# Output transposes of a hybrid attention and delta-rule block: on VectorE, between stores and 128-byte loads, instead of on TensorE

## The chip, the core and the metric

The kernel runs on one core of one Trainium2 chip. A core has five engines that run at the same time, each through its own list of instructions: TensorE (PE, matmuls), VectorE (DVE), ScalarE (ACT), GpSimd (POOL) and SyncE (SP, which issues the DMAs here). They hand work to each other through semaphores, and 16 DMA engines move data between HBM and the on-chip memory (SBUF: 128 partitions; matmuls write to PSUM). The metric is the device time of one execution in microseconds (us); of several runs the median is given.

## The reference

One block of a model: T = 1024 tokens of width D = 1024, all in float32. The normalized input is projected to the inputs of 8 heads of stick-breaking attention (64 wide) and of 4 heads of a gated delta rule (128 wide). Each head's output is normalized, multiplied by a gain and by a gate, and all go through one output projection, to which the input is added. A last norm ends it.

```python
h = rmsnorm(x, norm1_w[layer])
proj = jnp.einsum('btd,de->bte', h, w_in[layer])
sb_q, sb_k, sb_v, sb_z, g_q, g_k, g_v, g_z, g_b, g_a = jnp.split(proj, split_idx, axis=-1)
o_sb = stick_breaking_attention(...)
o_sb = rmsnorm(o_sb.transpose(0, 2, 1, 3), sb_norm_w[layer]).reshape(b, t_len, SB_WIDTH)
o_sb = o_sb * jax.nn.silu(sb_z)
...
o_gdn = gated_delta_chunked(gq, gk, gv, decay, beta)
o_gdn = rmsnorm(o_gdn.transpose(0, 2, 1, 3), gdn_norm_w[layer]).reshape(b, t_len, GDN_WIDTH)
o_gdn = o_gdn * jax.nn.silu(g_z)
mixed = jnp.concatenate([o_sb, o_gdn], axis=-1)
x = x + jnp.einsum('bte,ed->btd', mixed, w_out[layer])
...
return rmsnorm(x, final_norm_w)
```

## The kernel before, in words

**Matmuls.** A float32 product is made of three matmuls of the faster type `fp32r`: each operand is split in a high and a low half, and high x high, low x high and high x low are summed in PSUM (`mm3`). ACT makes a high half by copying to fp32r, DVE or POOL the low half by subtracting. A matmul of 128 x 512 results is the unit of nearly all work.

**Stages.** (1) The projections run through 24 groups of columns in the order of `ORDER`; they are the fill work of the whole span up to the last 60 us. (2) The delta rule (`gdn_*`): 4 heads, 8 chunks of 128 tokens; a unit is a head and half of its chunks (g = 0 or 1). `gdn_chain` walks the chunks of a unit one after the other, since each needs the state that the chunk before it left. Its output for a chunk is copied out of PSUM by ACT (`goe`) and stored to the DRAM array `og_s`; the factor of its norm is kept in `rsg`. (3) Attention (`window`): a head's queries in 4 windows w of 256. At a window's end the output lies in PSUM transposed (the head's 64 columns along the partitions, in two partial sums one above the other): ACT and DVE bring both halves together in `o2`, two transposes on PE turn it (`otf`), DVE's `tensor_reduce` adds the two partial sums (`oe`), and one DMA stores it to `o_s` in runs of 256 bytes. (4) The output projection runs over 8 blocks b of 128 tokens, first the delta rule's half (`products_delta`, blocks d0 to d7), then attention's (`products_attention`, a0 to a7): per block 2 halves of 512 columns x 4 rows of weights (k = 0 to 3) x 3 matmuls, so 24.

**A block's input.** `enter_delta` loads a block from `og_s` and its gate from `gate_s` into a place of `kq`, and scales each head by `rsg` on DVE (4 instructions). `enter_attention` loads from `o_s`, and norms with a square (ACT), a reduce (DVE), a power (POOL) and a product (DVE, by `rsb`). `prepare` and `split` then turn the block with 4 transposes on PE (`mwf`), multiply by the gate on DVE (`mf`), and make the halves `mh` (ACT) and `ml` (POOL). The product is added to the residual rows `xr` on DVE.

**The last weights.** `out_rows` loads the raw weight rows (`wor`) for both halves of the projection into the places sg1 and sg2 that attention's windows have left; `weight` makes `woh` (ACT) and `wol` (DVE) of them. The four rows of attention's half are made by `out_weights_attention` while the projection is under way.

**What sets the order.** The kernel is written as streams (Python generators with a priority, lines 1613 to 1619). At build time `interleave` runs them against a cost model of the engines (`Model`); at each point the ready stream with the lowest number emits its next piece. The order in which an engine begins its work in this model is then fixed by dependencies (line 1621), so PE, DVE, ACT, POOL and the DMA queue of SP all run through a list that the build has set. `flags` name events of the plan (`d3`: the add of the delta rule's block 3 was emitted; `e73`: the store of head 7's window 3). `Fixed` holds places in SBUF that several tensors use one after the other: sg0 to sg3, `o2`, and four of 4096 bytes per partition, `kq`. Every engine instruction goes through one helper, so the profile has them all at L359, and names tell them apart.

## Time and profile before

| | |
|---|---|
| runs of the kernel before | 640.44, 641.15, 641.22 us; median 641.15 |
| the profiled execution | 641.73 us, of it the span 639.8 us |
| instructions in the span | 11363 |
| DMA over the span | 116.01 MB, mean 181 GB/s |
| packets under 512 bytes | 53952 of 127162 |
| clock granted to PE | 9 of 9 tenths in 39 slices of 40, 8 in the last |

The span is what the profiler saw between the first and the last instruction; the execution's own time is 1.93 us longer. The rows that the prediction shows come from five views: the busy times and the chain that ended last (on the page), the waits of an engine (who waited for whom: total, times, longest), groups of like instructions (busy us, mean ns of one, then idle time before them and what ended it), the timeline (start, duration, instruction) and windows (busy time of each engine in a stretch, then the clock granted to PE, the DMA share and GB/s). DMA rows tell packets, MB and the share of the time of 16 engines; an issue row tells the count, the KB of one and the us from issue to landing.

### The profile page before, as it was taken

What the parts mean: (1) busy time and instruction counts of PE and PEld (TensorE: products, weight loads), DVE (VectorE), ACT (ScalarE), POOL (GpSimd) and SP (SyncE); (2) the same over time, 40 slices, a digit from 0 to 9 for tenths busy, and PEclk for the clock granted to TensorE, in tenths of its full rate; (3) what the DMA queues carried; (4) which work ended last, traced back from release to release, by engine and by line L of the source; (5) the groups of instructions that cost most, each with busy time, mean ns of one, the idle gap of its engine ahead of it and who ended that gap; (6) DMA issues with size and microseconds to landing.
All of it is one profiled execution on the core that took longest, in us unless ns stands there. A gap on an engine that the chain in (4) does not pass through costs nothing.

```text
span 639.8 us, 11363 instructions
## 1 busy us (share of the span) xinstructions
PE 630.5 (99%) x3768; PEld 536.1 (84%) x3768; DVE 443.1 (69%) x818; ACT 394.3 (62%) x945; POOL 340.3 (53%) x429
## 2 busy tenths in 40 slices
PE   8999999999999999999999999999999999999995
PEld 7889988998888888878888878888888888888885
DVE  4369973322797877886787868577878877567854
ACT  5755567724786776766687674575678753222553
POOL 0124047828694596865497763777353532246432
PEclk9999999999999999999999999999999999999998
DMA  8967338866456437787449674434253289833132
GB/s 296 352 204 288 121 133 255 284 214 211 137 151 232 121 91 221 172 222 240 123 115 256 177 226 125 139 113 167 77 161 98 81 288 358 309 99 98 67 131 100
DMA packets 127162, 116.01 MB, mean 181 GB/s; under 512 B 53952, under 2 KB 93056, under 8 KB 127104
## 3 DMA queue, kind: packets, MB, share of 16 engines
q1 hardware_dynamic: 126816, 115.09, 57.0%
q8 instruction: 30, 0.49, 0.3%
q14 instruction: 28, 0.23, 0.1%
q10 hardware_dynamic: 288, 0.20, 0.1%
HBM read 78.12 MB, written 37.13 MB: 180 GB/s over the span
## 4 chain that ended last, share of the span: by engine, by line
PE 90%; DVE 3%; ACT 3%; POOL 1%; DMA 1%; issue 1%; POOLq 0%; DVEq 0%; ACTq 0%; SPq 0%
PE pp L359 54%; PE pz L359 25%; PE po L359 7%; PE pc L359 3%; DMA cb<-cum_s 1%; DVE cc L359 1%; DVE pp L359 1%; ACT pre L359 1%; DMA n<-n 1%; ACT pz L359 0%; POOL ac L359 0%; DVE ahl L359 0%; POOL dt L359 0%; DVE ac L359 0%; ACT sgf L359 0%
## 5 line engine op out<-in xcount | busy, mean ns | idle before, releaser
L359 PE MATMUL pp<-xh,weh 128*128 128x512 f32 x360 | 145.8, 405 | 0.0
L359 PE MATMUL pp<-xh,wel 128*128 128x512 f32 x360 | 141.2, 392 | 0.0
L359 PE MATMUL pp<-xl,weh 128*128 128x512 f32 x360 | 140.6, 391 | 0.0
L359 POOL TENSOR_TENSOR sgf<-sgf,cc 128x128 f32<-128x128 f32 (+3 forms) x64 | 77.2, 1211 | 60.1 <-DVE cc L359 57.4
L359 POOL TENSOR_TENSOR wel<-wer,weh 128x512 fp32r<-128x512 f32 x48 | 63.3, 1321 | 47.8 <-ACT weh L359 47.6
L359 PEld LDWEIGHTS pp<-xh,wel 128*128 128x128 f32 x360 | 67.6, 188 | 15.2
L359 PEld LDWEIGHTS pp<-xh,weh 128*128 128x128 f32 x360 | 67.6, 188 | 12.1
L359 PEld LDWEIGHTS pp<-xl,weh 128*128 128x128 f32 x360 | 67.8, 188 | 11.8
L359 DVE TENSOR_TENSOR_SCAN cc<-pz,step 128x384 f32<-128x384 f32 (+2 forms) x64 | 53.5, 847 | 14.6 <-ACT pz L359 10.6
L359 ACT ACTIVATE sgf<-pz,rs 128x384 f32<-128x384 f32 (+3 forms) x96 | 53.6, 591 | 2.8 <-PE pz L359 2.5
L359 DVE TENSOR_TENSOR ahl<-pz,ahl 128x512 fp32r<-128x512 f32 (+1 forms) x80 | 49.6, 630 | 3.9 <-ACT ahl L359 3.3
L359 ACT ACTIVATE pz<-pz,ns 128x384 f32<-128x384 f32 (+3 forms) x96 | 52.1, 571 | 0.0
L359 ACT ACTIVATE ahl<-pz 128x512 fp32r<-128x512 f32 (+1 forms) x80 | 43.0, 557 | 12.1 <-PE pz L359 11.6
L359 PE MATMUL po<-ahl,v2a 128*128 128x512 f32 (+1 forms) x160 | 49.2, 402 | 0.0
L359 POOL TENSOR_TENSOR ml<-mf,mh 128x512 fp32r<-128x512 f32 x16 | 21.8, 1360 | 48.0 <-ACT mh L359 48.0
L359 POOL TENSOR_TENSOR ac<-ac,pre 128x512 f32<-128x512 f32 x24 | 30.9, 1289 | 27.3 <-ACT pre L359 24.2
L359 DVE SCALAR_TENSOR_TENSOR pp<-pre,conv,pp 128x512 f32<-128x512 f32 x42 | 31.5, 749 | 18.0 <-ACT pp L359 17.7
L359 DVE TENSOR_TENSOR_SCAN cc<-pz,cc,step 128x512 f32<-128x512 f32 (+1 forms) x32 | 38.8, 1212 | 5.4 <-ACT pz L359 4.2
L359 PE MATMUL pp<-wo,mh 128*128 128x512 f32 x128 | 40.7, 399 | 0.0
L359 PE MATMUL pz<-kh,q 128*128 128x384 f32 (+3 forms) x96 | 36.0, 382 | 0.1
L359 PEld LDWEIGHTS pz<-step,stf 128*128 128x128 f32 x288 | 30.8, 141 | 5.5 <-DVE cc L359 0.6
L359 ACT ACTIVATE weh<-wer 128x512 fp32r<-128x512 f32 x48 | 30.4, 636 | 5.8 <-PE pp L359 2.6
(302 smaller groups left out, 1571.2 us busy)
## 6 DMA issues: line engine op xcount, KB each, us to landing
wer<-wE SPq DMA_DIRECT2D x48, 256.0 KB, 3.3
xr<-x SPq DMA_DIRECT2D x16, 512.0 KB, 6.5
g_s<-ac SPq DMA_DIRECT2D x20, 256.0 KB, 2.2
v_s<-v2e SPq DMA_DIRECT2D x16, 256.0 KB, 3.0
kqf<-g_s SPq DMA_DIRECT2D x16, 256.0 KB, 3.6
v2a<-v_s SPq DMA_DIRECT2D x8, 512.0 KB, 4.2
q<-qk_s SPq DMA_DIRECT2D x8, 512.0 KB, 5.7
kh<-qk_s SPq DMA_DIRECT2D x8, 512.0 KB, 4.3
```

Source lines behind the costliest of these rows:

```text
L359: ins = f(*args, **kw).ins
```

## The change

- **Window's end.** The two PE transposes and the reduce go. DVE turns `o2` in 32 x 32 blocks (one instruction, 128 x 256), and four stores of 32 partitions each put the blocks in their transposed places in `o_s`, in runs of 128 bytes. Both partial sums are stored, side by side; `o_s` is twice as large.
- **`out_norm`, new.** Two streams share the 8 blocks. A block (512 KB) is loaded once all windows of the last head are stored, into the place of sg3, which is cut in two; DVE adds the partial sums, ACT squares, DVE reduces, POOL takes the power, DVE multiplies and turns in 32 x 32 blocks, and a store in runs of 256 bytes puts it to `on_s`.
- **`enter_attention`.** Four loads in runs of 128 bytes from `on_s` bring a block in transposed form; the norm is done already.
- **Delta rule.** `gdn_chain` copies its output into the unit's own place in `kq`; at the unit's end DVE scales all four chunks (one instruction) and turns them into the place of `kn`, and four stores in runs of 128 bytes write `og_s` in transposed form. `enter_delta` loads it as it is, without scaling; its first four blocks may come when the chain of unit 6 (units are 0 to 7) is done (flag c6), the others after the last chain (g).
- **`split`.** No transposes; the gate is multiplied in place, and `mh` and `ml` go to a place of `ak` (four of them; three buffers before).
- **Places.** `kn` and `at` share a place of the new fixed set `ak`, 4 x 4096 bytes.
- **Rules of the streams.** A raw row of attention's weights is loaded only after flags d1 to d4; the residual rows wait for d0 on (from the fourth block); the sigmoid and the product of `g_evac` get another priority, and so do `enter_x` and `out_norm`.

```diff
@@ window
-            op = pz()
-            ot = fx.words(o2, "ot")
-            for i in range(2):
-                TE.transpose(op[:, i * P:(i + 1) * P].bitcast(F32R), ot[:, i * P:(i + 1) * P], idr)
-            oe = at_.tile([P, 2, SBD], F32, tag="oe", bufs=2, name="oe")
-            V.tensor_reduce(oe, op[:, 0:256].rearrange("p (i u d) -> p i d u", i=2, u=2), AX.X, ALU.add)
-            flags[f"e{h}{w}"] = S.dma_start(o_s[2 * w:2 * w + 2, :, h * SBD:(h + 1) * SBD].rearrange("b t d -> t b d"), oe)
+            oe = at_.tile([P, 256], F32, tag="oe", bufs=2, name="oe")
+            V.transpose(oe, o2)
+            rows_o = o_s[256 * w:256 * w + 256, h].rearrange("(b r) d -> r b d", r=32)
+            flags[f"e{h}{w}"] = [S.dma_start(rows_o[:, :, 32 * a:32 * a + 32], oe[32 * a:32 * a + 32].rearrange("r (b c) -> r b c", c=32)) for a in range(4)]
...
+        def out_norm(n):
+            yield lambda: f"e{SBH - 1}3" in flags and fx.room("sg3")
...
+                both = fx.tile([P, SBH, 2, SBD], F32, "both", "sg3")
+                ck.hold(both)
+                yield S.dma_start(both.rearrange("p h u d -> p (h u d)"), o_s[b * P:(b + 1) * P].rearrange("t h d -> t (h d)"))
+                o, spare = both[:, :, 0, :], both[:, :, 1, :]
+                V.tensor_tensor(o, o, spare, ALU.add)
+                A.activation(spare, o, AF.Square)
...
+                V.tensor_tensor(o, o, ss.unsqueeze(2).to_broadcast([P, SBH, SBD]), ALU.mult)
+                V.transpose(spare, o)
+                ck.free(both)
+                flags[f"o{b}"] = S.dma_start(on_s[b].rearrange("p (n d) -> p n d", d=SBD), spare)
@@ gdn_chain
-                    oe = gd.tile([P, P], F32, tag="goe", bufs=2, name="goe")
-                    A.activation(oe, ob, AF.Copy)
-                    S.dma_start(og_s[c, :, h, :], oe)
+                    A.activation(og[:, j, :], ob, AF.Copy)
...
-            st["done"] = rsqrt(rsg[:, h, 4 * g:4 * g + 4], sso, 4)
+            st["done"] = rsqrt(rsg, sso, 4)
+            V.tensor_tensor(og, og, rsg.unsqueeze(2).to_broadcast([P, 4, P]), ALU.mult)
+            V.transpose(ogt, og)
+            for a in range(4):
+                ks = slice(32 * a, 32 * a + 32)
+                S.dma_start(og_s[4 * g:4 * g + 4, :, h, ks].rearrange("c (b r) t -> r (c b) t", r=32), ogt[ks].rearrange("r c (b t) -> r (c b) t", t=32))
+            ck.free(kq, kn, nkv)
@@ out_rows
-                    yield lambda: fx.room(f"sg{1 + n % 2}")
+                    yield lambda: fx.room(f"sg{1 + n % 2}") and (n < 4 or f"d{n - 3}" in flags)
@@ split
-            tp = pz()
-            mw = fx.words(mg, "mw")
-            yield from turned(tp, [mw[:, 0, j * P:(j + 1) * P] for j in range(4)])
-            fv = pools[0].tile([P, 512], F32, tag="mf", name="mf")
-            V.tensor_tensor(fv, tp, gt.rearrange("p k t -> p (k t)"), ALU.mult)
+            fv = mg[:, 0, :]
+            V.tensor_tensor(fv, fv, gt.rearrange("p k t -> p (k t)"), ALU.mult)
+            mm = fx.tile([P, 2, 4, P], F32R, "mm", "ak")
@@ enter_delta
-            yield lambda: "pool0" in flags and "z7" in flags
+            yield lambda: "z7" in flags
...
-                yield lambda: fx.room("kq")
+                yield lambda: ("c6" if b < 4 else "g") in flags and fx.room("kq")
...
-                for g in range(GH):
-                    gs = slice(g * P, (g + 1) * P)
-                    r = V.tensor_scalar(mx[:, gs], mx[:, gs], rsg[:, g, b:b + 1], None, ALU.mult)
@@ enter_attention
-                S.dma_start(mx, o_s[b])
...
+                for j in range(4):
+                    r.append(S.dma_start(mx[32 * j:32 * j + 32].rearrange("p (k a c) -> p k a c", k=4, a=4), heads[j]))
```

How the built order moves, at three places. VectorE, at the split of the last weight rows (`wol3`), before: `pp_7016` and `pp_7030` are the two halves of delta block 3, `pp_7082` is the first half of block 4.

```order
L359 SCALAR_TENSOR_TENSOR wol2_7000<-worf169_6896,mixw_67,woh2_6999 128x1024
L359 TENSOR_TENSOR xr_6859<-pp_7016,xr_6859 128x512
L359 TENSOR_TENSOR xr_6859<-pp_7030,xr_6859 128x512
L359 TENSOR_TENSOR mf_7076<-pz_7070,mgf167_6821 128x512
L359 SCALAR_TENSOR_TENSOR wol3_7041<-worf173_6994,mixw_67,woh3_7040 128x1024
L359 TENSOR_TENSOR xr_6861<-pp_7082,xr_6861 128x512
```

The same place of the change: `pp_7102` is the second half of the last delta block, d7, and `pp_7116` the first half of a0, the first block that uses `wol3`; `mgf169` and `mgf171` are inputs of attention's blocks, `bothf170` is a block of `out_norm`.

```order
L363 TENSOR_TENSOR xr_6991<-pp_7102,xr_6991 128x512
L363 TENSOR_TENSOR mgf169_6979<-mgf169_6979 128x512
L363 TENSOR_TENSOR mgf171_7000<-mgf171_7000 128x512
L363 TENSOR_TENSOR bothf170_6985<-bothf170_6985 128x8x64
L363 TENSOR_REDUCE oss_7136<-bothf170_6985 128x8
L363 TENSOR_SCALAR oss_7136<-oss_7136 128x8
L363 SCALAR_TENSOR_TENSOR wol3_7150<-worf172_7027,mixw_67,woh3_7149 128x1024
L363 TENSOR_TENSOR bothf170_6985<-bothf170_6985,oss_7136 128x8x64
L363 STREAM_TRANSPOSE bothf170_6985<-bothf170_6985 128x8x64
L363 TENSOR_TENSOR xr_6700<-pp_7116,xr_6700 128x512
```

`wol3` has moved from between blocks 3 and 4 of the delta half to behind its last add, and the first steps of a block of `out_norm` stand ahead of it. On ScalarE `woh3` stands right behind the square of the same `bothf170`.

SyncE's DMA queue, up to the load of the last weight rows (`worf173`), before: `mgf` with `og_s` and `gate_s` are a delta block's input, `fnw` is the final gain.

```order
L359 DMA xr_6867<-x 128x1024
L359 DMA gate_s_91<-zt_6852 128x512
L359 DMA worf169_6896<-wo 128x1024
L359 DMA mgf171_6924<-og_s_95 128x512
L359 DMA mgf171_6924<-gate_s_91 128x4x128
L359 DMA fnw_6964<-fnw 128x1024
L359 DMA worf173_6994<-wo 128x1024
```

And of the change, where the last weight rows are `worf172`:

```order
L363 DMA bothf166_6950<-o_s_94 128x1024
L363 DMA mgf167_6955<-gate_s_91 128x4x128
L363 DMA mgf167_6955<-on_s_95 32x16x32 x4
L363 DMA mgf169_6979<-gate_s_91 128x4x128
L363 DMA mgf169_6979<-on_s_95 32x16x32
L363 DMA xr_6991<-x 128x1024
L363 DMA mgf169_6979<-on_s_95 32x16x32 x3
L363 DMA mgf171_7000<-gate_s_91 128x4x128
L363 DMA mgf171_7000<-on_s_95 32x16x32 x4
L363 DMA bothf170_6985<-o_s_94 128x1024
L363 DMA worf172_7027<-wo 128x1024
```

The last weight rows now stand behind the residual rows of block 7 (`xr_6991`), inputs of attention's first blocks and two loads of `out_norm`.

TensorE, near the end of the delta rule, before: a window's end, between matmuls of the delta rule (`vr`, `pc`) and of attention's values (`po`).

```order
L359 MATMUL pz_6424<-state_6248,kqf89_4636 128x128
L359 MATMUL pz_6424<-vr_6315,at_4748 128x128
L359 MATMUL pz_6431<-step_65,otf145_6432 128x128 x2
L359 MATMUL po_6438<-ahl_6295,v2a_6326 128x512 x2
L359 MATMUL po_6438<-ahl_6403,v2a_6326 128x512
```

A like place of the change, where the last part of a window (`ahl` with `v2a`) is followed by a projection.

```order
L363 MATMUL pz_6455<-state_6374,kqf82_4270 128x128
L363 MATMUL pz_6455<-vr_6413,akf83_4273 128x128
L363 MATMUL pc_6469<-state_6436,kqf96_4732 128x128
L363 MATMUL po_6368<-ahl_6425,v2a_6113 128x512
L363 MATMUL po_6368<-ahl_6425,v2a_6113 128x2x128
L363 MATMUL pp_6484<-xh_112,weh_6327 128x512
```

The transposes with `otf`, as those with `mwf`, are gone from the list. Behind the delta rule's last matmul 27 projection matmuls stand before the first of the output projection; before there were 90.

79 lines of the change are left out of this document (43 added, 36 removed).

## The prediction

> **What bounds the kernel now.** First the page's busy times and the chain that ended last, then the waits of TensorE (PE).
>
> ```profile
> PE 630.5 (99%) x3768; PEld 536.1 (84%) x3768; DVE 443.1 (69%) x818; ACT 394.3 (62%) x945; POOL 340.3 (53%) x429
> PE 90%; DVE 3%; ACT 3%; POOL 1%; DMA 1%; issue 1%; POOLq 0%; DVEq 0%; ACTq 0%; SPq 0%
> PE po L359 <- DVE step L359: 1.7, 1, 1.7
> PE pp L359 <- DVE v2e L359: 0.4, 1, 0.4
> 616.38 16.81 PE pp L359 x84
> ```
>
> PE is busy for 630.5 of 639.8 us. Of the 9.3 us it is not, 1.7 lie at the start, and 6.6 at the end: the last row of PE in the chain of waits runs from 616.38 to 633.2, and the span ends at 639.8. The second largest wait is 0.4. So the kernel is as long as PE's list of instructions plus a fixed head and tail: a matmul that goes is worth its time on PE in full, work added to another engine is worth nothing until PE waits for it, and each wait that appears counts in full. The profiled execution took 641.73 us, 1.93 more than its span and 0.58 more than the median; I sum against 641.73 and take off the 0.58 at the end.
>
> **What the change removes from PE.** The durations of pipelined matmuls overlap, so I count from start to start.
>
> ```profile
> 507.68 0.37 PE L359 MATMUL pz<-step,otf 128*128 128x128 f32 x2
> 507.89 0.46 PE L359 MATMUL pp<-xh,weh 128*128 128x512 f32 x1
> 508.18 0.39 PE L359 MATMUL pp<-xl,weh 128*128 128x512 f32 x1
> 508.41 0.39 PE L359 MATMUL pp<-xh,wel 128*128 128x512 f32 x1
> ...
> 586.70 0.46 PE L359 MATMUL pz<-step,mwf 128*128 128x128 f32 x4
> 587.00 0.46 PE L359 MATMUL pp<-woh,mh 128*128 128x512 f32 x1
> 587.30 0.39 PE L359 MATMUL pp<-wol,mh 128*128 128x512 f32 x1
> ...
> 521.05 0.29 PE L359 MATMUL pz<-step,otf 128*128 128x128 f32 x2
> 521.17 0.50 PE L359 MATMUL pz<-step,mwf 128*128 128x128 f32 x4
> L359 PE MATMUL pz<-step,otf 128*128 128x128 f32 x64 | 11.4, 260 | 0.0
> L359 PE MATMUL pz<-step,mwf 128*128 128x128 f32 x64 | 7.4, 238 | 0.0
> ```
>
> A pair of attention's transposes (otf) takes 0.21 (507.68 to 507.89), and the matmul behind it 0.29 (to 508.18) where its neighbour takes 0.23 (508.18 to 508.41): 0.27 a pair, and the 64 of the group are 32 pairs, 8.6. Four transposes of a block's input (mwf) take 0.30, and the matmul behind them 0.30 instead of 0.23: 0.37, 16 times, 5.9. Together 14.5. Where the two kinds stand side by side, as at 521.05, the late start of a next matmul is counted twice; I take off 0.5: **−14.0**. The busy times of the groups (11.4 + 7.4 = 18.8) overlap with their neighbours and would be too much.
>
> **What it adds elsewhere.** VectorE (DVE):
>
> ```profile
> L359 DVE STREAM_TRANSPOSE wc<-xc 128x256 f32<-128x256 f32 x4 | 1.7, 428 | 0.0
> L359 DVE STREAM_TRANSPOSE pre<-ac 128x512 f32<-128x512 f32 x12 | 8.5, 707 | 5.4 <-POOL ac L359 5.4
> L359 DVE TENSOR_REDUCE oe<-pz 128x128 f32<-128x256 f32 x32 | 13.3, 416 | 2.6 <-PE pz L359 2.5
> L359 DVE TENSOR_SCALAR mgf<-mgf,rsg 128x128 f32<-128x128 f32 x32 | 8.0, 312 | 0.0
> L359 DVE TENSOR_TENSOR mgf<-mgf,rsb 128x512 f32<-128x512 f32 x8 | 7.7, 961 | 7.3 <-POOL rsb L359 7.3
> L359 DVE TENSOR_TENSOR xr<-pp,xr 128x512 f32<-128x512 f32 x31 | 21.3, 686 | 14.6 <-PE pp L359 14.3
> ```
>
> The window's transpose of 256 elements (0.43) takes the place of the reduce (0.42). New are 16 transposes of 512 elements (0.71), 8 adds of the two partial sums and 8 scalings of the delta rule's output (0.69 to 0.96 each); the 32 scalings by rsg (8.0) go. That is 11.4 + 11 to 15 − 8.0, some 15 to 20 us on an engine that is idle for 200, spread over the span beside PE: I cost it at nothing there. ScalarE and GpSimd (POOL) keep their counts. The sync engine (SP) issues some 136 more DMAs (128 stores of a window instead of 32, 32 loads of attention's output instead of 8, and a load and a store of the sums for each block); during attention nothing on PE waits for them soon, since the sums are first read in the last 60 us. If that cover is gone, what it costs is a wait of PE at the output projection, which I now work out.
>
> **What becomes late.** In the changed order only 27 projection matmuls stand between the delta rule's last matmul and the output projection, where 90 stood before; 63 x 0.23 = 14.5 us of cover are gone while the list of transfers is longer.
>
> ```profile
> 520.00:560.00 40.00, 40.00 (x191) 32.78 (x190) 26.17 (x54) 13.87 (x19) 10.82 (x8) 1.00 0.94 335
> 560.00:600.00 40.00, 40.00 (x191) 32.63 (x191) 27.96 (x45) 11.69 (x23) 21.57 (x15) 1.00 0.31 91
> DMA packets 9860, 14.88 MB, mean 338 GB/s; under 512 B 1198, under 2 KB 5907, under 8 KB 9855
> q1 hardware_dynamic: 9855, 14.82, 95.0%
> 564.25 1.28 DVE L359 SCALAR_TENSOR_TENSOR wol<-worf,mixw,woh 128x1024 fp32r<-128x1024 f32 x1
> L359 DVE SCALAR_TENSOR_TENSOR wol<-worf,mixw,woh 128x1024 fp32r<-128x1024 f32 x4 | 5.2, 1304 | 1.7 <-ACT woh L359 1.7
> L359 ACT ACTIVATE woh<-worf,mixw 128x1024 fp32r<-128x1024 f32 x4 | 4.5, 1142 | 0.0
> L359 ACT ACTIVATE sq<-mgf 128x512 f32<-128x512 f32 x8 | 5.0, 626 | 11.6 <-DVE ssb L359 9.5 <-DMA mgf<-o_s 2.1
> ```
>
> In the second column from the right the DMA engines are full (0.94) from 520 to 560 and nearly free (0.31) from 560 to 600. The last weight rows (k = 3) were split on DVE at 564.25 and first needed after 587.00, over 21 us ahead. This margin is what the change spends.
>
> (a) By the order. Let E be the end of the last delta product on PE. PE reaches the rows k = 3 nine matmuls later, at E + 2.1. On DVE stand ahead of that split, after E: the add of the last product (0.69), two products with the gates (2 x 0.69), the add of both partial sums (0.96, as the strided scaling above). On ACT the square (0.63) and the high half (1.14) follow, then DVE's low half (1.30). Sum 6.1; five handovers, 0.5 together by my allowance: E + 6.6. The wait is 6.6 − 2.1 = 4.5.
>
> (b) By the transfers. For the price of 128-byte runs I take the stores of the delta rule's turned inputs, which the kernel before already makes:
>
> ```profile
> DMA packets 1284, 0.16 MB, mean 80 GB/s; under 512 B 1280, under 2 KB 1284, under 8 KB 1284
> q1 hardware_dynamic: 1284, 0.16, 52.2%
> gt_s<-pre SPq DMA_DIRECT2D x48, 64.0 KB, 2.8
> ```
>
> These are 2 us, from 250: 0.16 MB took 52.2% of 2 us of all 16 engines, 0.42 us per 64 KB; the 14.82 MB above, from 516 to 560, took 95.0% of 44 us, 2.82 us per MB. Between the delta rule's end and the load of the last weight rows SP's new order issues 17 transfers of 512 KB, 18 of 256 KB (13.6 MB) and 20 of 64 KB in 128-byte runs: 13.6 x 2.82 + 20 x 0.42 = 47 us, or 49 with the engines 95% full. The first of them waits until the last unit's output was scaled and turned, about 5 us (my estimate, from 1.0 of the pow on POOL, 0.69, 0.71 and handovers) and about 1.5 to start. E comes after 27 + 8 x 24 matmuls, 50.4 us after the delta rule's end; the rows land at 6.7 + 47 to 49, so E + 3.3 to 5.3, and both halves of the split (2.4) make them ready at E + 5.7 to 7.7: a wait of 3.6 to 5.6. It is not added to (a): the later of the two counts. I take **+5.0**; the bounds are 0, if the transfers start sooner or hide better than in these rows, and 15 (below).
>
> (c) The first half of delta block 4 finds its weight rows behind the same kind of queue on DVE, an add of 0.69 behind a split: **+0.6**, bounds 0 and 2.
>
> (d) A PE that pauses does not return at full speed:
>
> ```profile
> 634.00:636.00 2.00, 0.00 (x0) 0.00 (x0) 1.18 (x4) 0.62 (x1) 0.78 (x2) 0.79 0.10 37
> 636.00:640.00 4.00, 0.00 (x0) 0.00 (x0) 0.00 (x0) 0.00 (x0) 0.00 (x0) 0.50 0.35 131
> 5.72 0.63 PE L359 MATMUL pz<-xh,wqh 128*128 128x512 f32 x1
> 6.15 0.63 PE L359 MATMUL pp<-xh,wql 128*128 128x512 f32 x1
> ...
> 7.00 0.45 PE L359 MATMUL pp<-xl,wqh 128*128 128x512 f32 x1
> 7.29 0.39 PE L359 MATMUL pz<-xl,wqh 128*128 128x512 f32 x1
> ```
>
> The third column from the right is the granted clock: after the last matmul at 633.2 it averages 0.79 from 634 to 636 and 0.50 after, a fall about 2 us into the pause (0.79 is 1.16 us at 1 and 0.84 at 0.5). At the start the matmuls stand 0.43 apart until 7.0, 5.3 us after the first, and 0.23 behind it. So a pause of 5 us would be followed by up to 5.4 us at half speed, a loss of **+2.7**; bounds 0 (the clock holds) and 2.7.
>
> The Trainium skill, "TensorE: Matmul & The Clock Gate", section "Part 1: The HAM clock gate (the "warmup" mystery)", has the gate fall after an idle window of about 3.4 us and open again after about as long of work: the loss would be half of 3.4, an estimate of 1.7, and the sum would come out 1.0 lower. That the gate falls in a pause the row of 0.50 agrees with; the duration differs.
>
> The Trainium skill, "DMA: Bandwidth & Descriptors", section "Specifications", speaks against the change: under 512 bytes a transfer falls below line rate, and the engine reads, modifies and writes. The rows agree: 0.42 us for 64 KB in 128-byte runs against 0.18 at 2.82 us per MB. With runs at line rate the list in (b) would be 4.7 us shorter, and (a) alone would set the wait, 0.5 less than I take.
>
> **Sum.** −14.0 + 0.6 + 5.0 + 2.7 = −5.7: 641.73 − 5.7 = 636.0 against the profiled execution, **635.4** against the median.
>
> **The rivals.** *Nothing is late*: the last rows come at most 2 us after E, since transfers overlap better than in the full stretch. Then only −14.0 and at most the small terms stay: 627.1 to 632. For it: the DMA engines were two thirds idle from 560 on. Against: both (a) and (b) give a wait on their own. *The pause comes, the clock holds*: −14.0 + 0.6 + 5.0, 632.7; it lies within my forecast's band. *Deeper*: the delta blocks too wait for inputs or weights, 3 to 4 us more with a second fall of the clock: 638 to 639.9. For it: loads of block inputs stand among the 47 us. *Slower*: SP issues in order, and a load of what was just stored (the turned outputs from the DRAM copies) must wait at the queue's head until the store has landed, 2.8 us by the stores' row, while nothing behind it starts. Four such drains would be 4 x 2.7 = 10.8 us on the path of (b): a wait of 15.8 instead of 5.0, 646.2. Slower decides itself once the wait at k = 3 passes 10.7 us (14.0 − 0.6 − 2.7). Against it: the order puts other loads between most stores and their loads. *The change does not do what it says* can be excluded: neither kind of transposes is left in PE's order.
>
> **How the numbers follow.** The forecast, 632 to 638, has 0.50; nothing late (under 632) 0.20; deeper (638 to 639.9) 0.10; within 0.2% of 641.15 (about what a measurement of this kernel can tell from no change) 0.08; slower 0.12. So faster 0.80, same 0.08, slower 0.12. The range 627.0 to 641.5 takes in the full saving and stops short of the slower case: what it leaves out is 0.13 above and about 0.04 below.
>
> **What would show it.** Right: PE idles some 5 us just before its first matmul with the low half of the last weight rows, nine matmuls into the first attention block, at about 575 to 582; the wait names DVE's low half, which itself stands behind the add of the last delta product; the granted clock dips in the slice behind; the DMA share is 0.9 for 45 us ahead of it; the tail behind the last matmul stays 6.6. PE's busy time falls by 13 to 14 plus what half speed adds. Wrong: no pause of PE above 2 us (the transfers then started sooner than I take), a pause without a dip, more than one large pause, or SP waiting at its queue's head for stores.

## The result and the profile after

The changed kernel takes 644.45 us (median of 5 runs, 643.25 to 646.62) against 641.15 us before (640.44 to 641.84): a ratio of 1.0054, 95% interval 1.0042 to 1.0066. The prediction was 635.4, with a range up to 641.5. The profiled execution took 643.69, with a span of 642.0; it lies 0.76 below its median, where the one before lay 0.58 above.

First the page of the changed kernel: busy times, the chain that ended last by engine, and the DMA queue.

```profile
PE 623.2 (97%) x3640; PEld 527.6 (82%) x3640; DVE 455.0 (71%) x818; ACT 394.1 (61%) x945; POOL 341.4 (53%) x429
PE 77%; DMA 7%; SPq 5%; ACT 4%; DVE 4%; issue 2%; POOL 1%; POOLq 0%; DVEq 0%; ACTq 0%
DMA packets 190780, 124.41 MB, mean 194 GB/s; under 512 B 121664, under 2 KB 156672, under 8 KB 190720
q1 hardware_dynamic: 190432, 123.48, 66.0%
```

PE has 128 instructions less and is busy for 7.3 us less, but it now idles 18.8 us of the span, where it was 9.3. DMA and SyncE's queue together have 12% of the chain, where they had 1%; PE has 77% where it had 90%. Packets rose by half (127162 before), bytes by 7% (116.01 MB before). The waits of PE name two places:

```profile
PE pp L363 <- ACT woh L363: 5.6, 1, 5.6
PE po L363 <- DMA v2a<-v_s: 1.7, 1, 1.7
```

The first is the pause at the last weight rows. The timeline of PE there, and the pieces of the chain ahead of it (start, duration, what):

```profile
583.55 0.40 PE L363 MATMUL pp<-woh,mmf 128*128 128x512 f32 x1
589.54 0.80 PE L363 MATMUL pp<-woh,mmf 128*128 128x512 f32 x1 [5.59 <-ACT woh L363]
590.86 0.80 PE L363 MATMUL pp<-wol,mmf 128*128 128x512 f32 x1 [0.53 <-DVE wol L363]
591.45 1.05 PE L363 MATMUL pp<-woh,mmf 128*128 128x512 f32 x2
...
594.01 0.67 PE L363 MATMUL pp<-woh,mmf 128*128 128x512 f32 x2
594.52 0.39 PE L363 MATMUL pp<-wol,mmf 128*128 128x512 f32 x1
...
576.67 4.72 DMA mgf<-on_s
...
583.22 5.09 DMA worf<-wo
...
588.34 1.16 ACT woh L363
...
589.52 1.30 DVE wol L363
```

The load of the last rows starts at 583.22, behind inputs of attention's blocks that come through `on_s`, and lands at 588.3; the high half takes 1.16 more. PE stands for 5.8 us, then runs at about 0.43 a matmul in place of 0.23 until 594.0. From 589.54 to 594.01 are 8 steps, 4.5 us where 1.9 are usual, 2.6 more, of which 0.5 is the wait for the low half: 8.4 us for the place. Windows of the changed kernel (second column from the right: DMA share) show what stands behind it:

```profile
540.00:560.00 20.00, 20.00 (x88) 16.12 (x87) 13.62 (x23) 4.21 (x6) 7.64 (x5) 1.00 0.98 299
560.00:580.00 20.00, 20.00 (x88) 16.12 (x87) 11.44 (x16) 5.36 (x7) 6.64 (x5) 1.00 0.93 254
580.00:590.00 10.00, 4.04 (x16) 2.56 (x14) 6.50 (x10) 3.04 (x4) 4.03 (x4) 0.86 0.92 230
```

The DMA engines are full to 590; before, their share fell to 0.31 from 560 on. The second place is in attention's stage: the chain's piece of the load, and the timeline of PE.

```profile
361.10 6.67 DMA v2a<-v_s
...
367.81 0.61 PE L363 MATMUL po<-ahl,v2a 128*128 128x512 f32 x2 [1.75 <-DMA v2a<-v_s]
...
368.82 0.76 PE L363 MATMUL pp<-xh,weh 128*128 128x512 f32 x1
369.38 0.63 PE L363 MATMUL pp<-xl,weh 128*128 128x512 f32 x1
...
371.51 0.63 PE L363 MATMUL pz<-kh,q 128*128 128x512 f32 x1
371.94 0.53 PE L363 MATMUL pz<-kl,q 128*128 128x512 f32 x1
372.30 0.33 PE L363 MATMUL pz<-kh,q 128*128 128x384 f32 x1
```

A wait of 1.75 us, and half speed from 368.8 to 371.9: 7 steps in 3.1 us where 1.6 are usual. Together some 3.4 us.

Last, what the removed transposes were worth. From start to start, summed over the trace of before, the otf transposes took 6.2 and the mwf ones 4.8: 11.0, not 14.0. A place like the one at 507.54 to 508.18 before, where two `pc` matmuls, the pair and a projection followed each other, reads in the changed kernel:

```profile
521.76 0.38 PE L363 MATMUL pc<-xct,xinv 128*128 128x128 f32 x2
521.90 0.48 PE L363 MATMUL pp<-xh,weh 128*128 128x512 f32 x1
522.21 0.40 PE L363 MATMUL pp<-xl,weh 128*128 128x512 f32 x1
```

The pair is gone, and the matmul behind still takes 0.31 (521.90 to 522.21): here the late start belongs to any short matmul ahead, and another short one stands there now. In the trace of before 9 of the 32 pairs had such a projection matmul behind them and 15 a `po` matmul that starts as late, and so did the matmuls behind the 16 groups; how many of these late starts went can't be read from one place. The sum can: PE idles 9.5 us more in the span, half speed takes 3.7 us from its matmuls (half of 3.4 us near 370 and of the 4.0 us that PE worked at it from 589.5 on), and the span grew by 2.2. That leaves 11.0 by which PE's list itself became shorter, no more than the transposes' own time.

The spans' difference, +2.2, is then −11.0 + 8.4 + 3.4, and 1.4 in pieces of under 0.7 each.

### The profile page after: what moved, and what is told of

It is laid out like the page before. It is cut to its first block, busy times and chain, and to the rows that moved or that the text cites. A ratio compares the mean times of both kernels' runs of the same rounds, so it can differ in the third digit from the quotient of the medians.

```text
span 642.0 us, 11269 instructions
## 1 busy us (share of the span) xinstructions
PE 623.2 (97%) x3640; PEld 527.6 (82%) x3640; DVE 455.0 (71%) x818; ACT 394.1 (61%) x945; POOL 341.4 (53%) x429
## 4 chain that ended last, share of the span: by engine, by line
PE 77%; DMA 7%; SPq 5%; ACT 4%; DVE 4%; issue 2%; POOL 1%; POOLq 0%; DVEq 0%; ACTq 0%
PE pp L363 45%; PE pz L363 22%; PE po L363 6%; SPq L363 5%; PE pc L363 3%; DMA xr<-x 2%; DVE cc L363 1%; DMA v2a<-v_s 1%; DMA kh<-qk_s 1%; DMA worf<-wo 1%; ACT sgf L363 1%; DMA mgf<-on_s 1%; DMA og_s<-akf 1%; POOL mmf L363 1%; ACT pz L363 1%
## 5 line engine op out<-in xcount | busy, mean ns | idle before, releaser
L363 PE MATMUL pp<-xh,weh 128*128 128x512 f32 x360 | 146.5, 407 | 0.4 <-DVE ac L363 0.4
L363 PE MATMUL pp<-xh,wel 128*128 128x512 f32 x360 | 141.8, 394 | 0.0
L363 PE MATMUL pp<-xl,weh 128*128 128x512 f32 x360 | 141.0, 392 | 0.0
L363 POOL TENSOR_TENSOR sgf<-sgf,cc 128x128 f32<-128x128 f32 (+3 forms) x64 | 77.5, 1216 | 57.7 <-DVE cc L363 52.7
L363 POOL TENSOR_TENSOR wel<-wer,weh 128x512 fp32r<-128x512 f32 x48 | 62.8, 1311 | 73.4 <-ACT weh L363 71.0
L363 PEld LDWEIGHTS pp<-xh,wel 128*128 128x128 f32 x360 | 67.9, 189 | 15.3
L363 PEld LDWEIGHTS pp<-xh,weh 128*128 128x128 f32 x360 | 67.9, 189 | 12.6 <-DVE ac L363 0.8
L363 PEld LDWEIGHTS pp<-xl,weh 128*128 128x128 f32 x360 | 68.1, 189 | 11.5
L363 DVE TENSOR_TENSOR_SCAN cc<-pz,step 128x384 f32<-128x384 f32 (+2 forms) x64 | 53.4, 844 | 10.6 <-ACT pz L363 9.5
L363 ACT ACTIVATE sgf<-pz,rs 128x384 f32<-128x384 f32 (+3 forms) x96 | 53.5, 593 | 9.2 <-PE pz L363 9.2
L363 DVE TENSOR_TENSOR ahl<-pz,ahl 128x512 fp32r<-128x512 f32 (+1 forms) x80 | 49.5, 630 | 12.3 <-ACT ahl L363 11.7
L363 ACT ACTIVATE ahl<-pz 128x512 fp32r<-128x512 f32 (+1 forms) x80 | 43.2, 560 | 20.6 <-PE pz L363 20.1
L363 ACT ACTIVATE pz<-pz,ns 128x384 f32<-128x384 f32 (+3 forms) x96 | 52.5, 576 | 0.0
L363 PE MATMUL po<-ahl,v2a 128*128 128x512 f32 (+1 forms) x160 | 48.9, 400 | 1.8 <-DMA v2a<-v_s 1.7
L363 PE MATMUL pp<-woh,mmf 128*128 128x512 f32 (+2 forms) x136 | 42.5, 394 | 6.0 <-ACT woh L363 5.6
L363 PE MATMUL pp<-wo,mmf 128*128 128x512 f32 x192 | 44.8, 395 | 0.0
L363 POOL TENSOR_TENSOR mmf<-mgf,mmf 128x512 fp32r<-128x512 f32 x16 | 22.0, 1379 | 42.3 <-ACT mmf L363 39.5
L363 DVE SCALAR_TENSOR_TENSOR pp<-pre,conv,pp 128x512 f32<-128x512 f32 x42 | 31.4, 748 | 18.2 <-ACT pp L363 17.8
L363 PEld LDWEIGHTS pp<-wo,mmf 128*128 128x128 f32 x192 | 36.0, 188 | 8.6
L363 DVE TENSOR_TENSOR_SCAN cc<-pz,cc,step 128x512 f32<-128x512 f32 (+1 forms) x32 | 38.8, 1212 | 5.9 <-ACT pz L363 4.7
L363 POOL TENSOR_TENSOR ac<-ac,pre 128x512 f32<-128x512 f32 x24 | 31.0, 1292 | 15.5 <-ACT pre L363 9.8
L363 DVE TENSOR_TENSOR xr<-pp,xr 128x512 f32<-128x512 f32 (+2 forms) x33 | 22.2, 672 | 23.5 <-PE pp L363 23.4
```

Of the source, the lines that this page charges most:

```text
L363: ins = f(*args, **kw).ins
```

## The experiments

All ratios are to the kernel before, run on the same chip; "the changed kernel" is at 1.0054.

| run | median us (range) | ratio, 95% interval |
|---|---|---|
| e1 weights early | 640.93 (638.47–643.47) | 0.9992 (0.9978–1.0007) |
| e2 window, long runs | 645.74 (640.96–648.60) | 1.0057 (1.0036–1.0078) |
| e3 blocks, long runs | 639.90 (638.31–643.96) | 0.9982 (0.9970–0.9995) |
| e4 window on PE | 646.95 (645.82–649.42) | 1.0094 (1.0077–1.0112) |
| e5 cover 78 | 649.90 (648.98–651.90) | 1.0129 (1.0114–1.0144) |
| e6 cover 3 | 643.82 (641.25–648.20) | 1.0041 (1.0021–1.0060) |
| e7 cover 78, weights early | 650.59 (649.71–652.22) | 1.0139 (1.0125–1.0152) |
| e8 stores on ScalarE | 662.42 (658.61–665.57) | 1.0320 (1.0284–1.0355) |
| e9 blocks, long runs, weights early | 637.34 (635.60–638.99) | 0.9936 (0.9918–0.9953) |
| e10 one store a window | 645.50 (641.03–653.34) | 1.0068 (1.0042–1.0094) |
| e11 attention's blocks on PE, weights early | 637.93 (636.34–642.75) | 0.9950 (0.9935–0.9966) |
| e12 window only | 641.15 (638.32–643.29) | 0.9995 (0.9980–1.0009) |
| e13 as e11, values first | 638.67 (637.73–643.91) | 0.9962 (0.9946–0.9977) |
| e14 values first | 654.46 (654.05–657.01) | 1.0206 (1.0191–1.0220) |
| e15 delta only | 643.86 (641.16–646.01) | 1.0049 (1.0033–1.0065) |

**e1: the last weights without their flags.**

```diff
-                    yield lambda: fx.room(f"sg{1 + n % 2}") and (n < 4 or f"d{n - 3}" in flags)
+                    yield lambda: fx.room(f"sg{1 + n % 2}")
```

> The raw weight rows of attention's half are loaded without waiting for the flags d1 to d4; TensorE's order stays the same, and the load of the last rows moves up by 12 places in SyncE's queue, past two loads of out_norm's blocks and the inputs of attention's blocks 1 to 3. Theory A (the pause at the last weight rows comes from their late load alone): the wait of 5.6 us and the half-speed stretch behind it go, 7.5 to 8.7 us less than the changed kernel's 644.5, so 636 to 637, faster than before by 0.7%. Rival B (the DMA queue as a whole is too long, whatever stands first): the wait moves to the inputs of attention's blocks or to the residual rows, and the time falls by less than 4 us, to 641 or more.

640.93. The wait at the last rows is gone and 3.5 us with it, less than half of what theory A gave. In their place PE waits in small pieces for other loads of the same list (total, times, longest): the residual rows `xr` and the blocks' inputs `mmf`.

```profile
PE pp L363 <- DVE xr L363: 2.3, 3, 1.2
PE pp L363 <- POOL mmf L363: 0.9, 2, 0.6
PE pp L363 <- ACT mmf L363: 0.5, 1, 0.5
```

So the rows were late because the list was too long, more than because of their place in it: rival B, for the larger part (640.93 lies just under its 641).

**e2 and e3: the same orders, longer runs.** In e2 only the window's stores, in e3 only the blocks' stores and loads; the planner still counts runs of 128 bytes, so no engine's order moves.

```diff
-            rows_o = o_s[256 * w:256 * w + 256, h].rearrange("(b r) d -> r b d", r=32)
...
+            at = 256 * w + 32 * h
...
+            flags[f"e{h}{w}"] = [S.dma_start(o_s[at + 8 * a:at + 8 * a + 8].rearrange("r h (u d) -> (r h u) d", u=1).rearrange("(r m) d -> r (m d)", m=2), oe[32 * a:32 * a + 32]) for a in range(4)]
```

```diff
-                S.dma_start(og_s[4 * g:4 * g + 4, :, h, ks].rearrange("c (b r) t -> r (c b) t", r=32), ogt[ks].rearrange("r c (b t) -> r (c b) t", t=32))
...
+                S.dma_start(og_s[4 * g:4 * g + 4].rearrange("c p h t -> c (p h) t")[:, P * h + 32 * a:P * h + 32 * a + 32].rearrange("c r t -> r c t"), ogt[ks])
...
-                    r.append(S.dma_start(mx[32 * j:32 * j + 32].rearrange("p (k a c) -> p k a c", k=4, a=4), heads[j]))
...
+                    r.append(S.dma_start(mx[32 * j:32 * j + 32], on_s[b, 32 * j:32 * j + 32]))
```

> The stores at a window's end keep their number, bytes and place in every engine's order, but write runs of 1 KB in place of 128 bytes, so attention's outputs land in the wrong places of the scratch array. Theory A (the short runs keep the DMA engines busy, and a load of attention's values lands late: the wait of 1.7 us near 366 with its half-speed stretch): that wait goes, 2.5 to 4 us less than the changed kernel, 640.5 to 642; the pause at the last weight rows stays. Rival B (the number of DMAs in SyncE's queue does it, not their runs): no change beyond 1 us, 643.5 to 645.5.

> The four stores of a delta unit's turned output write runs of 512 bytes and the four loads of an attention block's input read runs of 2 KB, in place of 128 bytes; number, bytes and every engine's order stay, and blocks get the wrong elements. Theory A (the pause at the last weight rows is bound by the time the transfers take): 20 transfers of 64 KB ahead of them cost about 0.2 us each in place of 0.42, the rows land some 4 us earlier, the wait falls from 5.6 to under 2.5, and the time by 4 to 7 us, to 637.5 to 640.5. Rival B (bound by the order on VectorE and by SyncE's issuing): the wait falls by less than 1 us, the time stays above 643.

e2 changes nothing (645.74, 0.2 above rival B's band): the wait for `v2a` is still 2.0 us in its profile. So the short runs of the window's stores aren't what delays that load. e3 falls to 639.90; in its profile the wait at the last rows is less than half:

```profile
PE pp L364 <- ACT woh L364: 2.4, 1, 2.4
PE pp L364 <- DVE wol L364: 1.1, 1, 1.1
```

The instructions, bytes and orders are the changed kernel's; only the time that the transfers of the blocks take has changed. That is theory A of e3: in the changed kernel the time of the transfers bounds the pause. What is left of it in e3 is something else. SyncE's queue and ScalarE there:

```profile
572.73 0.38 SPq L364 DMA_DIRECT2D worf<-wo  x1
...
581.18 0.61 ACT L364 ACTIVATE bothf<-bothf 128x512 f32<-128x512 f32 x1
581.70 1.13 ACT L364 ACTIVATE woh<-worf,mixw 128x1024 fp32r<-128x1024 f32 x1
```

The rows, issued at 572.73, land at 577.5, before PE begins a0 at 578.2 (in the changed kernel they land 6.7 us behind that point). ScalarE makes the high half only at 581.70, right behind the square of a block of `out_norm`, and the low half is ready at 584.65, 6.6 us after the last delta product's end at 578.0. That is count (a) of the prediction, the order alone, with its own 6.6. Not all of e3's gain lies here, either: its pause begins 3.4 us earlier in the span than the changed kernel's, of the spans' difference of 5.2, for one because the wait for `v2a`, 1.3 us, has no half speed behind it in this execution.

**e4: the window's end on TensorE again.** The lines that the change took out at a window's end are back, with `o_s` as before; `out_norm` loads `o_s[b]` (256 KB) and doesn't add.

> Only the window's end is as before (two transposes on TensorE, one store in runs of 256 bytes); the rest of the change stays, and out_norm loads 256 KB a block without the add. Theory A (the window's part of the change saves 6.2 us on TensorE and costs some 4 us of waits in attention's stage, and its larger loads some of the pause): 6.2 more, 4 less, and 1 to 2 less at the pause: 644 to 646, within 0.3% of the changed kernel. Rival B (the stores in short runs cost more than the transposes saved): 641 or less. Rival C (they cost nothing, the waits come from the planner's order): 649 or more.

646.95, 2.5 us above the changed kernel: theory A's sum of gain and cost fits (644 to 646) but for 1 us. The order moved, though: in its profile PE waits 3.2 us for an input of an attention block at 623, so the number is no clean price of the window's part.

**e5, e6, e7: the cover.** One constant of the planner changes its order; the instructions are the same.

```diff
-HOPS = {"A": 145, "G": 75, "P": 197, "V": 130, "S": 900}
+HOPS = {"A": 145, "G": 75, "P": 197, "V": 130, "S": 850}
```

In e6 it is `cost = 500` for `cost = 475`; e7 is e5 with e1's edit.

> The same instructions as the changed kernel; only one constant of the planner is another (the hop after a DMA, 850 in place of 900), and its order then leaves 78 projection matmuls behind the delta rule's last matmul in place of 27. Theory A (the pause at the last weight rows is the list of transfers less its cover): 51 x 0.23 = 11.8 us more cover than before against a pause of 6.7 with its half speed, so the pause goes, 8 to 9 us less than the changed kernel: 634.5 to 638. Rival B (the transfers' own number and form, wherever they begin, hold up the output projection): the wait comes back at other loads, 641 or more.

> Again the same instructions, with another constant (500 for an issue of SyncE in place of 475): the order leaves 3 projection matmuls behind the delta rule's last one in place of 27. Theory A: 24 x 0.23 = 5.5 us less cover, a pause longer by as much: 648 to 652. Rival B (the cover doesn't matter): within 2 us of the changed kernel, 642.5 to 646.5.

> The order with 78 matmuls of cover, and attention's weight rows loaded without waiting for flags d1 to d4. Theory A: the pause is gone by the cover already, so this adds nothing: within 1.5 us of the kernel with the cover alone. Rival (both are needed, or the early weights delay the block inputs): over 2 us away from it, to either side.

Theory A, as a statement on the time, falls in both directions: 78 matmuls of cover give 649.90, 3 give 643.82. With 78 the wait at the last weight rows is gone, as it said, but PE waits elsewhere in the output projection:

```profile
PE pp L363 <- DVE xr L363: 4.8, 2, 4.1
PE pp L363 <- ACT wo L363: 2.8, 1, 2.8
```

These are the residual rows and the last rows of the delta half; with 3, PE waits 3.4 us for `xr` and 1.7 for `woh`. In e5's profile the DMA share is 0.91 from 500 to 520 already, where it is 0.59 in the changed kernel, so the added cover is no free time for transfers there. But each constant moves the whole order, not the cover alone, so these runs don't price the cover by itself. e7 (650.59) is within 1.5 us of e5, as said, though not because the waits are gone: PE waits 4.3 us for a block's input and 2.4 for weight rows of the delta half.

**e8 and e10: fewer issues of SyncE.** In e8 ScalarE issues the window's stores, at the place where the planner had SyncE begin them; in e10 one store of 128 partitions in runs of 1 KB stands for the four, with the planner's orders kept.

```diff
+    def side(self, out, src):
+        op = self.model.record("S", self.model.A.real.dma_start(out, src).ins, [out], [src], cost("S", "dma_start", (out, src), {}), None)
+        op.side = True
+        return op
...
-        self.order[eng].append(op)
+        self.order["A" if op.side else eng].append(op)
...
```

> The changed kernel with every other order the same; the 128 stores at the windows' ends are issued by ScalarE, at the place in its order where the planner had them begin, in place of SyncE. Theory C (the wait of 1.7 us for attention's values, and the half speed behind it, come from SyncE's issuing, which has no gap from 338 to 361): that wait goes, 2.5 to 4 us less, 640.5 to 642. Rival D (the DMA engines, not the issuing): the wait stays, and the time is within 1.5 us of 644.5, or longer where ScalarE's issuing holds up its own work.

> The changed kernel with every engine's order the same, but the four stores at a window's end are one store of 128 partitions in runs of 1 KB (attention's outputs land in the wrong places): 96 issues of SyncE less, the same bytes. Theory C (the wait of 1.7 us for attention's values and its half speed come from the number of issues): they go, 640.5 to 642. Rival D (its place in the order, or the DMA engines): the wait stays, 643.5 to 646.

e8 is 18 us slower than the changed kernel. The wait for `v2a` isn't in its profile, but that at the last rows is (6.5 us), and the waits for results of ScalarE and VectorE are many (`cc` 3.0, `ahl` 2.7, `wy` 1.9 us), so it says little on the question. e10 does: 96 issues less, and the wait stays, 2.6 us in its profile, with 645.50. Theory C falls.

**e9: e1 and e3 together.**

> Two edits at once on the changed kernel: attention's weight rows are loaded without the flags, and the delta units' stores and the attention blocks' loads use runs of 512 bytes and 2 KB (blocks get the wrong elements). Each alone took 3.5 to 4.5 us of the loss away. Theory A (the DMA engines, full from 530 to 590, are the bound of the output projection; less time for the list and a better place for the last rows add up): all its waits go, 634.5 to 637.5. Rival B (the waits move to what the planner's order has late next): 639 or more.

637.34, 7.1 us below the changed kernel; what is left of waits in the output projection is 0.6 and 0.5 us. Shorter transfers and a better place of the last rows together clear it, in the range that theory A gave. Like e2, e3 and e10 this kernel puts elements in the wrong places; it stands for the time alone.

**e11: attention's blocks turned on TensorE.** The way through `on_s` goes: the block is normed, put into its place and turned by four transposes. e1's edit is in it too.

```diff
-                V.tensor_tensor(o, o, ss.unsqueeze(2).to_broadcast([P, SBH, SBD]), ALU.mult)
-                V.transpose(spare, o)
-                ck.free(both)
-                flags[f"o{b}"] = S.dma_start(on_s[b].rearrange("p (n d) -> p n d", d=SBD), spare)
...
+                r = V.tensor_tensor(mx.rearrange("p (h d) -> p h d", d=SBD), o, ss.unsqueeze(2).to_broadcast([P, SBH, SBD]), ALU.mult)
+                ck.free(both)
+                ready["in", b, 0] = mg, gt, [r]
...
+                if g == 0:
+                    yield lambda: ps.room("pz", 4)
+                    tp = pz()
+                    mw = fx.words(mg, "mw")
+                    yield from turned(tp, [mw[:, 0, j * P:(j + 1) * P] for j in range(4)])
+                    ready[b, g] = split(mg, gt, tp)
```

> On the changed kernel: attention's blocks are normed in place and turned by 4 transposes on TensorE as before, so out_norm's way through on_s (8 stores, 32 loads in short runs) goes; the weight rows are loaded early; the window's end and the delta rule's half stay as changed. TensorE has 8 x 0.30 to 0.37 = 2.4 to 3.0 us more. Theory A (the output projection waits for the DMA engines): its waits go, 644.5 - 8.7 + 2.7, so 637 to 640. Rival B (waits as in the changed kernel stay): 643 or more.

637.93, faster than before by 0.50% (0.34 to 0.65%), though PE has 32 transposes more than in the changed kernel. The windows of its profile, to be read against those of the changed kernel:

```profile
540.00:560.00 20.00, 20.00 (x87) 16.18 (x87) 12.28 (x15) 4.58 (x7) 4.86 (x3) 1.00 0.98 314
560.00:580.00 20.00, 20.00 (x90) 16.14 (x89) 11.71 (x17) 3.15 (x5) 7.15 (x5) 1.00 0.56 197
580.00:600.00 20.00, 20.00 (x95) 16.23 (x94) 14.84 (x25) 7.68 (x16) 8.33 (x7) 1.00 0.44 143
```

From 560 to 580 the DMA share is 0.56 in place of 0.93, and PE doesn't stop; its waits from 500 on are 0.3 and 0.2 us. Early rows alone gave 640.93 (e1) and left waits of up to 1.2 us; without the eight stores and 32 loads through `on_s` the time is 3.0 us lower, with 32 transposes more. A run without `on_s` and with late rows wasn't made.

**e12 and e15: one half of the change at a time.** e12 is the kernel before with the window's part (blocks load both sums, add, and are turned on TensorE); e15 has the delta rule's part, with attention as before.

> The kernel before with the window's part of the change alone (one buffer for the turned output in place of two): VectorE turns it, four stores in runs of 128 bytes, both partial sums are loaded and added ahead of the norm; all blocks are turned on TensorE as before. TensorE loses 32 x 0.19 = 6.2 us. Theory A (the stores in attention's stage are cheap, the loss is in the output projection's transfers): 636 to 638.5, faster than before by 0.5 to 0.8%. Rival B (these stores delay the delta rule's and attention's loads): 641 or more.

> The counterpart of e12: only the delta rule's half of the change (its output scaled and turned on VectorE, blocks loaded in transposed form) with its places in SBUF; attention's windows, blocks and weight loads as before. TensorE loses 8 x 0.30 to 0.37 = 2.4 to 3.0 us, and the list of transfers of the output projection is as long as before but for 32 stores in short runs. Theory A (what the change loses there is attention's way through on_s and the doubled sums): no waits over 1 us, 637.5 to 640. Rival G (the places shared in SBUF and the later end of the delta rule cost as much): 641 or more.

e12 comes out at 641.15, no change, the figure of rival B: 6.2 us of PE are given back, in its profile by waits for `xr` (2.7, in the output projection, with half speed behind it) and for `v2a` (1.4, in this order at 272), and smaller ones. So theory A's place is among them, with rival B's time. e15 comes out at 643.86, slower: rival G's figure. It has no `on_s`, no doubled sums and no wait for `v2a`, and yet its ratio (1.0049) is nearly the whole change's. Its profiled execution was its fastest, 641.16, and shows no wait over 0.7 us but that at the start; the small ones add up to 2.5 us, where before had 0.6, and take most of what the transposes gave. What makes the other five up to 4.9 us longer isn't in that profile, and isn't half speed, since their granted clocks are 0.996 to 0.998. It stays open.

**e13 and e14: attention's values first.** The load of `v2a` near 362 stands in SyncE's queue of the changed kernel behind seven others that it shares the DMA engines with; it took 6.67 us, where the quickest of these loads takes 4.2. Its stream gets the planner's first priority (the third argument; the lowest number comes first), in e13 on top of e11.

```diff
-Stream(attention_values(), 9.99, WINDOW)
+Stream(attention_values(), 9.99, OUT_WEIGHTS)
```

> The kernel with attention's blocks turned on TensorE and early weights (e11), in which the loads of attention's values get the planner's first priority, so that the load near 362 stands ahead of four loads of the delta rule (some 0.7 MB) in SyncE's queue. Theory E (the wait of 1.7 to 2.6 us there, and the half speed behind it, come from this load's place behind others that share the DMA engines with it, and not from the stores' runs or number): the wait goes, 2 to 4 us less than e11's 637.9: 634 to 636. Rival F (the priority only moves the wait to the delta rule's loads): within 1 us of e11 or above it.

> The changed kernel with that priority alone; its order leaves 51 projection matmuls behind the delta rule's last one in place of 27. Theory E with a DMA-bound output projection: the wait at attention's values goes (2 to 4 us less), the output projection keeps waits of 6 to 9 us: 640 to 642.5. Rival F: 643.5 to 646.

In e13 the wait for `v2a` is gone, and PE waits at the same time for the delta rule's `dt`, a load that now stands behind it:

```profile
PE pz L363 <- DVE dt L363: 1.3, 1, 1.3
```

638.67 against 637.93: rival F. In both orders tried a load of that stretch is late. e14 fits neither of its theories: 654.46, above the 646 of rival F. The wait for `v2a` is gone, one for `dt` has come (2.2 us), and SyncE's queue has stopped in the output projection. It is a relative of the prediction's slower rival, with a store that waits for its data in place of a load that waits for a store (timeline of SyncE, and what it waited for from 584 to 600):

```profile
585.05 0.94 SPq L363 DMA_DIRECT2D mgf<-gate_s  x2
595.22 0.35 SPq L363 DMA_DIRECT2D out<-xr  x1
596.83 4.16 SPq L363 DMA_DIRECT2D on_s<-bothf  x2
...
SPq L363 <- DVE xr L363: 9.2, 1, 9.2
```

The queue stands for 9.2 us before the store of a finished output block, and the stores and loads through `on_s` stand behind it in the queue. PE then waits twice for the input of a later block, 5.2 us to 611.9 and 8.2 to 634.8, 13.4 in all. That the first follows from this stop, and the second from a later one of the same kind, is read from the order of the issues; no run with these stores elsewhere was made.

## Why the prediction was wrong, step by step

- **"PE's list bounds, each wait that appears counts in full"**: right. The spans' difference of 2.2 us is what PE's list became shorter by, 11.0, against its added waits and half-speed stretches, 13.2.
- **"−14.0"**: mis-sized; measured, 11.0. The error was the step from one place to all: the 0.06 to 0.07 us of the next matmul's late start were booked as saved for every pair and group, from one example of each. The transposes' own time is all that PE's list lost; at the place shown the late start stayed, behind another short matmul. 3.0 of the 7.9 us by which the forecast of the span was short; the rest of the distance from 635.4 to 644.45 is where the two profiled executions lie against their medians.
- **"+5.0" and "+2.7" at the last weight rows**: right in place and cause, and close in size, 8.4 against 7.7, in part by luck: the waits were 1.3 longer and the half speed 0.6 shorter than said, since of a stretch of 6.8 us 2.3 passed in the pause already. Of the two counts the transfers (b) decided: the rows landed at 588.3, 6.7 us after the first matmul of a0 (3.3 to 5.3 by the forecast), and e3 shortens the wait by the transfers' time alone (e9 and e11 clear it, with early rows too). With the transfers shorter, count (a) is what remains in e3: "the later of the two counts" held.
- **The cover in (b)** ("63 x 0.23 = 14.5 us of cover are gone"): not borne out as a price. 3 and 78 matmuls of cover give waits in the output projection as well (e6, e5), at other loads; since each of these orders is new as a whole, how much the cover counts beside the list of transfers isn't shown.
- **(c) "+0.6"** at the first half of delta block 4: no such wait in the profile.
- **"During attention nothing on PE waits for them soon"**: this is the step that failed outright. The new DMAs were costed at nothing there since nobody reads the sums soon; but the planner, with 136 more DMAs, made a new order of everything, and in it a load of attention's values lands 1.75 us too late, with half speed behind it: 3.4 us. Longer runs (e2), fewer issues (e10) and another place of the load (e13) each leave a wait there; with the window's part alone (e12) there is such a wait elsewhere, with the delta rule's part alone (e15) none. That the planner's new order packs more into the DMA engines there than they can carry is the reading that fits; a run that changes the amount alone wasn't made, so it is argued, not shown.
- **Open.** e15 shows that the delta rule's half, which has neither of these two places, is as slow as the whole in the median. The account above is of one execution of each kernel, and no run here says where e15's loss lies.
- **The rivals**: "nothing is late" would have needed e9's or e11's list. The time fell where "slower" lay, but not by that mechanism: SyncE did stand once for a store to land (`SPq L363 <- DMA on_s<-bothf: 4.3, 1, 4.3`), before its issue at 590.0 and so behind the last rows, not on their path; its stands for `og_s` ahead of them come to 1.2 us. The prediction had named such stands as a sign against itself.

## What to carry to other kernels

Where TensorE is the bound, count a removed instruction at its own start-to-start time, and book a neighbour's late start only where nothing short is left ahead of it. Moving work off TensorE by way of DRAM costs DMA time in the stage where the data comes back: in the stage whose DMA share was 0.92 to 0.98 here, turning attention's blocks on chip was the faster way (e11), even at some TensorE time. And where a planner sets the order, a change of its inputs moves the waits of the whole kernel, so a stage that was "free" has to be read again. One profile is one execution: compare it with the runs' range before a median is explained by it.

## What the hardware showed unexpectedly

The half speed comes in steps, and not behind every wait. Granted clock (third column from the right) of the changed kernel, then of e10 (one line) and e11:

```profile
368.00:369.00 1.00, 1.00 (x10) 0.96 (x10) 1.00 (x4) 0.54 (x2) 0.98 (x1) 0.90 0.94 237
369.00:372.00 3.00, 3.00 (x9) 2.35 (x9) 3.00 (x8) 0.74 (x2) 3.00 (x4) 0.50 0.48 73
372.00:373.00 1.00, 1.00 (x6) 0.92 (x5) 0.82 (x2) 0.50 (x1) 1.00 (x2) 0.89 0.00 0
587.00:588.00 1.00, 0.00 (x0) 0.00 (x0) 0.33 (x1) 0.63 (x1) 1.00 (x1) 0.63 0.89 273
588.00:594.00 6.00, 3.94 (x8) 2.77 (x9) 4.11 (x6) 1.87 (x3) 2.09 (x2) 0.50 0.70 157
594.00:595.00 1.00, 1.00 (x6) 0.80 (x5) 0.57 (x1) 0.00 (x0) 0.00 (x0) 0.96 0.89 213
...
368.00:372.00 4.00, 4.00 (x23) 3.48 (x24) 4.00 (x12) 2.18 (x5) 3.88 (x4) 1.00 0.31 54
...
395.00:396.00 1.00, 1.00 (x36) 1.00 (x31) 0.66 (x2) 0.98 (x6) 0.00 (x0) 0.76 0.72 259
396.00:402.00 6.00, 6.00 (x32) 4.87 (x30) 2.92 (x8) 3.70 (x18) 2.09 (x6) 0.50 0.63 180
```

In the changed kernel the clock is at a half for 3.4 us (0.2 + 3 + 0.2), from 368.8 on, a microsecond after PE had taken up work again, and for 6.8 us from 587.3 on, which begins in the pause. In all traces here a stretch that ends in full speed lasts 3.4, 6.8 or 10.2 us. The Trainium skill, "TensorE: Matmul & The Clock Gate", section "Part 1: The HAM clock gate (the "warmup" mystery)", counts activity in windows of about 3.4 us: the stretches agree with it, one, two and three windows, but a wait of 1.75 us was enough here, half a window.

The length of the wait alone does not decide. At the same load e10 waited 2.6 us and kept its clock (1.00 from 368 to 372), and in e11 the clock fell at 395.5 with no wait of PE from 370 to 403, behind some 3 us of mostly 32 x 32 matmuls. One reading is an estimate from the stretches' own beat: counted back in steps of 3.41 us from e10's stretch at 585.2, its wait is cut at 366.8 into 1.4 and 1.2 us, while the 1.75 of the changed kernel lie within one step (365.4 to 368.8). It isn't the whole rule: e6 kept its clock with 1.7 us within one step (364.1 to 367.5).

This shows in the runs. Before, 29 runs lie within 640.58 to 642.08, while e2's 12 lie within 640.96 to 648.60, with the instructions all alike. The mean granted clock goes with it: 0.992 in e2's fastest run and 0.982 in its slowest, at most 6.4 of the 7.6 us; in e11 0.999 (636.34) and 0.987 (642.75). The profiled executions of e2 and e10 are among their fastest, those of e1 and e11 are their slowest, and these two hold a stretch of half speed near 395, where the changed kernel's profile has none.
